# Own rows of the two large groups copied on GpSimd's queue, those of the third made by two products, first one-hots two units later

## Chip, cores and metric

The kernel runs on one NeuronCore of a Trainium2 chip. The metric is the time of one execution in device microseconds (us), lower is better; a measured time is the median of several executions. TensorE is called PE, VectorE DVE, ScalarE ACT, GpSimd POOL and SyncE SP. PE is granted one of two clocks, 2.4 or 1.2 GHz, which the profile shows as 1.00 and 0.50.

## What is computed

Two transformer-like blocks over 256 tokens of width 1024, in float32, each a mixer of attention and recurrence followed by a PEER layer. The change lies in the PEER layer, which both blocks have. For each token it makes queries for 8 heads, scores them against two sets of 128 sub-keys, takes the best 16 of each, then the best 16 of their sums, and so picks 16 of 16384 experts per head. Each expert is one row of `u` and one row of `v`:

```python
q = (xb @ w_q).reshape(B, T, PEER_HEADS, 2, PEER_DKEY // 2)
s1 = jnp.einsum('bthd,nd->bthn', q[..., 0, :], k1); s2 = jnp.einsum('bthd,nd->bthn', q[..., 1, :], k2)
v1, i1 = lax.top_k(s1, PEER_TOPK); v2, i2 = lax.top_k(s2, PEER_TOPK)
...
top_s, pos = lax.top_k(cand_s, PEER_TOPK)
idx = jnp.take_along_axis(cand_i, pos, axis=-1)
g = jax.nn.softmax(top_s, axis=-1)
h = jnp.einsum('bthkd,btd->bthk', jnp.take(u_tab, idx, axis=0), xb)
a = gelu(h) * g
return jnp.einsum('bthk,bthkd->btd', a, jnp.take(v_tab, idx, axis=0))
```

## The kernel before

The function `peer` computes the layer in two ways at once. The first 104 tokens are served by gathered rows. They lie in three groups, `GROUPS = ((2, 0), (4, 64), (16, 96))`: tokens 0 to 63 with each token on 2 partitions, 64 to 95 on 4, and 96 to 103 on 16. POOL fetches the chosen `u` rows and later the `v` rows by indirect DMA, 104 fetches of 128 rows each (512 KB), and DVE multiplies a fetched `u` row with the token's own normed row, which stands in `xg[:, g, :]` on every partition that serves that token (line 1103). The other 152 tokens are served densely: PE multiplies them with all of `u` and all of `v`, and the choice of experts comes in as a gate matrix, made from one-hot rows of the two indices (`one_hots`, `one_hots_by_gate`, `gate_product`, `gate_apply`), in 38 blocks of 4 tokens.

The layer has three stages on PE. In the query stage, 32 units of `w_q` are used: the loop runs `t` over two halves of the tokens and `hc` over 16 halves of heads; each turn multiplies one unit (512 KB of weights, `query`), ACT copies the product into `qts` (line 1332), PE scores the turn before last (`score`, line 1302), and after every second score ACT copies the scores to `s_all` (line 1305). In the `u` stage the dense tokens meet 128 units of `u` (line 1427), with the gate products between them; in the `v` stage they meet 128 units of `v` (line 1484). SP loads all the units in order into seven buffers, as they come free.

The routing (best 16, sums, decoding) is a Python generator that issues DVE work a piece at a time beside the units: `beside` gives it a budget per unit, and a `yield None` ends its turn for that unit. After heads 0 and 1 of the first half it calls `spread`, a few small PE products (line 1147) that bring the expert numbers `eif` (line 1265) onto the partitions of the groups; ACT copies them to `ei`, and POOL may then fetch rows. Three more spreads follow, after each two heads. When the routing has ended (`if not side`), the first block of one-hots is issued at the unit that is then reached; the remaining blocks are spaced evenly up to five units before the end of the stage. Before that a unit may use 0.5 gathered rows, after it 0.98 (`beside(2.45 if at else 2.07, 0.98 if at else 0.5)`). Rows that are not used by then are used in the `v` stage.

Own rows are made in the turns `t == 0`, `hc` 4 to 6: `gain` holds the first half's normed rows (line 1336), and `own_rows` issues 22 DMAs from ACT's queue inside SBUF, 2 of 256 KB, 4 of 128 KB and 16 of 32 KB. ACT issues them in its program's order, between its copies of `q` and of the scores.

Of the kernel before, what the change touches and what calls it, by code (L numbers as in the profile page):

```python
# [12 lines left out]
AF = mybir.ActivationFunctionType  # L13
# [38 lines left out]
def two_blocks_kernel(ctx: ExitStack, tc: tile.TileContext, a: dict, out: bass.AP, dbg=None, stop=None):  # L52
    nc = tc.nc
# [118 lines left out]
    def load_const(pool, name, shape, dt=F32):  # L172
        t = pool.tile(shape, dt, name="c_" + name)
        nc.gpsimd.dma_start(out=t, in_=a[name])
        return t
# [33 lines left out]
    def bank_b(name):  # L209
        return pp_b.tile([P, 512], F32, tag="b", name=name)  # L210
# [788 lines left out]
    def peer(which, norm, names, shared, gelu, after):  # L999
        keys_name, gain_name, u_rows, v_rows = names  # L1000
        with ExitStack() as es:
# [7 lines left out]
            xg = hp.tile([P, len(GROUPS), D], F32, name="xg")  # L1009
# [25 lines left out]
            gain = gp.tile([P, D], F32, tag="rows", name="gain")  # L1035
# [6 lines left out]
            ng = len(GROUPS)  # L1042
            sel = load_const(hp, "sel", [P, ng + sum(c for c in PARTS if c > 1), P])
# [119 lines left out]
            def scales_done(t):  # L1163
                nc.vector.reciprocal(rs[:, t:t + 1], rs[:, t:t + 1])

            def own_rows(g, qs):

                r, t0 = GROUPS[g]
                n = P // r
                for q in qs:  # L1170
                    nc.scalar.dma_start(out=xg[q * n:(q + 1) * n, g, :], in_=gain[t0:t0 + n, :])  # L1171

            def scales_by_column():

# [23 lines left out]
            def route_head(t, h):  # L1198

                for c in range(2):  # L1200
                    yield from best16(v_t[:, c, :], i_t[:, h, t, c, :], s_all[:, h, t, c, :], tmp, 320)
                v1, v2 = v_t[:, 0, :], v_t[:, 1, :]
                for o, a0, na, nb in ((0, 0, 1, 16), (16, 1, 3, 8), (40, 4, 4, 4), (56, 8, 8, 1)):
                    sh = [P, na, nb]
                    nc.vector.tensor_tensor(
                        cand[:, o:o + na * nb].rearrange("p (a b) -> p a b", a=na),
                        bc(v1[:, a0:a0 + na, None], sh), bc(v2[:, None, 0:nb], sh), op=ALU.add)
                yield 660
                yield from best16(top[:, t, h, :], pos[:, t, h, :], cand, tmp[:, 0:64], 270)
# [37 lines left out]
            def exps(t):  # L1247
                nc.vector.tensor_tensor(gt[:, t], top[:, t], bc(top[:, t, :, 0:1], m3), op=ALU.subtract)
                nc.scalar.activation(gt[:, t], gt[:, t], AF.Exp)

            def softmax(t):
                nc.vector.tensor_reduce(zs[:, t], gt[:, t], axis=AX.X, op=ALU.add)
                nc.vector.reciprocal(zs[:, t], zs[:, t])
                nc.vector.tensor_tensor(gt[:, t], gt[:, t], bc(zs[:, t, :, None], m3), op=ALU.mult)

            def routing():

                for h in range(8):
                    while not heads[0]:
                        yield None  # L1260
                    yield from route_head(0, heads[0].pop(0))
                    if h % 2:
                        yield from decode(0, h - 1, 2)
                        hs = slice(h - 1, h + 1)
                        nc.vector.scalar_tensor_tensor(
                            eif, fid[:, 0, 0, hs, :].rearrange("p h k -> p (h k)"), 128.0,
                            fid[:, 1, 0, hs, :].rearrange("p h k -> p (h k)"), op0=ALU.mult, op1=ALU.add)
                        w = G // 4
                        spread(eif, 2, ei[:, (h // 2) * w:(h // 2 + 1) * w])
                        fetch["known"] = h + 1  # L1270
                        fetch_rows()
                exps(0)
                for h in range(8):
                    while not heads[1]:
                        yield None
                    yield from route_head(1, heads[1].pop(0))
                    if h == 0:
                        softmax(0)
                        spread(gt[:, 0].rearrange("p h k -> p (h k)"), 8, gg)
                    if h == 3:  # L1280
                        yield from decode(1, 0, 4)
                exps(1)
                yield from decode(1, 4, 4)
                softmax(1)
                pts = [tpp.tile([P, 512], F32, tag="tp", name="pt") for c in range(2)] + [bank_b("pt")]
                for c, pt in enumerate(pts):
                    for t in range(2):
                        v = gt[:, t] if c == 2 else fid[:, c, t]
                        nc.tensor.transpose(pt[:, t * P:(t + 1) * P], v.rearrange("p h k -> p (h k)"), ident)
                yield None  # L1290
                for c, pt in enumerate(pts):
                    nc.scalar.activation(idx[:, c, :], pt[:, G:T], AF.Copy)

            sps = {}
            heads = [[], []]
# [30 lines left out]
            for t in range(2):  # L1326
                for hc in range(16):
                    q = query(t, hc)
                    if t == 0 and hc == 0:
                        square_sums(x_ss, 0, (1,))  # L1330
                        scales(0)
                    nc.scalar.activation(qts[hc % 4], q, AF.Copy)
                    if t == 0 and hc == 1:
                        scales_done(0)
                        to_plain(1, range(4, 8), norm)
                        nc.vector.scalar_tensor_tensor(gain, x_sb[:, 0, :], rs[:, 0:1], gain, op0=ALU.mult, op1=ALU.mult)
                        side.append(routing())
                    if hc > 1:
                        score(t, hc - 2)
                    elif t == 1:  # L1340
                        score(0, hc + 14)
                    if t == 0 and hc == 2:
                        square_sums(x_ss, 1, (1,))
                        scales(1)
                    if t == 0 and hc == 3:
                        scales_done(1)
                    if t == 0 and hc == 4:
                        own_rows(0, range(2))
                        own_rows(1, range(4))
                    if t == 0 and hc in (5, 6):  # L1350
                        own_rows(2, range(8 * hc - 40, 8 * hc - 32))
                    if t == 1 and hc == 8:
                        by_column = scales_by_column()
                    if t == 1 and 9 <= hc < 13:
                        scaled(by_column, 2 * (hc - 9))
                    beside(2.05, 0.3 * t)
# [74 lines left out]
            for n in range(NE):  # L1431
# [11 lines left out]
                if not side:  # L1443
                    start = at[0] if at else n
# [30 lines left out]
            for n in range(NE):  # L1475
# [7 lines left out]
                for d in range(KT):  # L1483
                    nc.tensor.matmul(  # L1484
                        block(d), lhsT=w[:, d * P:(d + 1) * P], rhs=XA[:, n, :], start=(n == 0 and d % nb == 0),
                        stop=(n == NE - 1), skip_group_check=True)
# [236 lines left out]
```

## Time and profile before

| what | value |
|---|---|
| median of 3 runs | 1810.66 us (1810.16 to 1813.28) |
| the profiled execution | 1809.62 us, of which the span from first to last instruction is 1807.5 us |
| mean granted PE clock | 0.987 |
| busy share of PE, DVE, ACT, POOL | 96%, 63%, 33%, 28% |
| first block: query, `u`, `v` stage on PE | 257.3 to 349.9, 349.9 to 652.3, 652.3 to 936.5 us |
| second block: the same | 1103.7 to 1203.0, 1203.0 to 1505.4, 1505.4 to 1795 us |

Busy shares are means over stages with different limits; the stage in which a thing lies decides what it is worth.

### The profile page before, as it was taken

The numbers are of one execution on the slowest core, as the hardware profiler recorded it, in microseconds if no ns is written. First come the engines' busy times: TensorE is split into PE (matmuls) and PEld (weight loads), VectorE is DVE, ScalarE is ACT, GpSimd is POOL, SyncE is SP. The second block draws the span as 40 slices with busy tenths as digits, with TensorE's granted clock in tenths as the row PEclk, the third lists the DMA queues.
The fourth block names the chain that finished last, engine by engine and source line by source line (L and its number), as shares of the span: only waits on it lengthen the run. The fifth ranks groups of instructions, "written<-read, shape, count | busy, mean of one in ns | idle before, by whom it ended". The sixth has DMA issues, their size and how long they took to land.

```text
span 1807.5 us, 32650 instructions
## 1 busy us (share of the span) xinstructions
PE 1736.6 (96%) x12460; PEld 1625.6 (90%) x12460; DVE 1135.1 (63%) x2698; ACT 594.5 (33%) x1643; POOL 500.1 (28%) x444
## 2 busy tenths in 40 slices
PE   8999996999999999999999998799999999999997
PEld 6778886999999999989988777799999999999997
DVE  5556657798677864445455543879777886444444
ACT  6665541322665520000017563132266651000001
POOL 0000001122344344444410000212244345444441
PEclk9999998999999999999999999799999999999999
DMA  7434568899999999999985227789999999999995
GB/s 267 140 118 139 179 215 275 297 358 396 385 411 418 405 411 419 419 418 419 419 311 186 94 84 251 263 288 367 387 395 412 418 402 419 419 419 419 418 419 219
DMA packets 162732, 591.74 MB, mean 327 GB/s; under 512 B 18528, under 2 KB 18688, under 8 KB 162320
## 3 DMA queue, kind: packets, MB, share of 16 engines
q1 hardware_dynamic: 99648, 362.07, 52.6%
q0 software_dynamic: 61424, 224.12, 31.2%
q10 hardware_dynamic: 1504, 3.48, 0.8%
q8 instruction: 98, 1.61, 0.3%
q14 instruction: 58, 0.48, 0.1%
HBM read 585.40 MB, written 1.05 MB: 324 GB/s over the span
## 4 chain that ended last, share of the span: by engine, by line
PE 75%; DMA 19%; DVE 2%; ACT 1%; issue 1%; ACTq 1%; SPq 0%; DVEq 0%
PE h L1427 29%; DMA raw<-in_v_dram 17%; PE y L1484 14%; PE q L1313 5%; PE pj L296 5%; PE pj L298 5%; PE pj L297 4%; PE g L1387 4%; DMA raw<-in_w_q_dram 2%; PE spread L1147 1%; ACTq L1171 1%; PE sps L1302 1%; PE sc L476 1%; PE hs L797 1%; PE fold L1124 0%
## 5 line engine op out<-in xcount | busy, mean ns | idle before, releaser
L1484 PE MATMUL y<-XA,raw 128*128 128x152 f32 x4096 | 556.6, 295 | 14.4 <-DMA raw<-in_v_dram 10.0
L1484 PEld LDWEIGHTS y<-XA,raw 128*128 128x128 f32 x4096 | 534.2, 190 | 39.3 <-DMA raw<-in_v_dram 34.0
L1427 PE MATMUL h<-un,raw 128*128 128x152 f32 x4096 | 544.0, 293 | 0.0
L1427 PEld LDWEIGHTS h<-un,raw 128*128 128x128 f32 x4096 | 533.0, 190 | 0.0
L1089 POOL DMA_INDIRECT rows<-in_u_rows_dram,ei x208 | 217.7, 1046 | 528.8 <-DVE hg L1103 296.4
L1089 POOL DMA_INDIRECT rows<-in_v_rows_dram,ei x208 | 267.3, 1285 | 316.4 <-DVE acc L1112 251.3
L1112 DVE SCALAR_TENSOR_TENSOR acc<-rows,ag,acc 128x1024 f32<-128x1024 f32 x202 | 259.4, 1284 | 3.1 <-DVE XA L1495 0.3
L1103 DVE CUSTOM_DVE_ANT_0 rows<-rows,xg 128x1024 f32<-128x1024 f32 x208 | 252.7, 1216 | 0.0
L116 ACT ACTIVATE hi<-raw 128x1024 fp32r<-128x1024 f32 (+1 forms) x109 | 114.3, 1052 | 338.7 <-PE y L1484 284.9
L1495 DVE MEMSET XA<- 128x1 f32 x128 | 7.6, 59 | 284.2 <-PE y L1484 258.0
L117 DVE TENSOR_TENSOR lo<-raw,hi 128x1024 fp32r<-128x1024 f32 (+1 forms) x109 | 131.5, 1212 | 84.6 <-ACT hi L116 83.9
L1313 PE MATMUL q<-act,raw 128*128 128x128 f32 x1024 | 138.8, 293 | 5.8 <-issue 5.0
L1313 PEld LDWEIGHTS q<-act,raw 128*128 128x128 f32 x1024 | 132.4, 208 | 6.8 <-issue 5.7
L296 PE MATMUL pj<-hi,act 128*128 128x512 f32 x320 | 131.7, 411 | 2.3 <-ACT hi L116 1.4
L298 PE MATMUL pj<-hi,act_l 128*128 128x512 f32 x320 | 125.8, 393 | 0.1
L297 PE MATMUL pj<-lo,act 128*128 128x512 f32 x320 | 125.7, 393 | 0.0
L1415 ACT ACTIVATE XA<-h 128x152 f32<-128x152 f32 (+37 forms) x252 | 65.4, 260 | 151.5 <-PE h L1427 147.8
L1036 POOL DMA_DIRECT2D gain<-in_gain_dram x2 | 1.1, 534 | 396.5 <-PE out L298 252.6
L1513 ACT ACTIVATE XA<-y 128x384 f32<-128x384 f32 (+1 forms) x6 | 2.5, 456 | 290.3 <-DVE XA L1512 290.3
L1392 DVE TENSOR_TENSOR XA<-g,XA 128x208 f32<-128x208 f32 (+18 forms) x76 | 40.2, 528 | 81.7 <-ACT b L1377 30.2
L1412 ACT ACTIVATE hb<-h 128x8 f32<-128x8 f32 (+37 forms) x152 | 38.2, 251 | 129.6 <-PE h L1427 119.5
L1387 PE MATMUL g<-b,b 128*128 128x128 f32 x608 | 80.1, 275 | 0.0
(367 smaller groups left out, 1814.6 us busy)
## 6 DMA issues: line engine op xcount, KB each, us to landing
raw<-in_u_dram SPq DMA_DIRECT2D x256, 512.0 KB
raw<-in_v_dram SPq DMA_DIRECT2D x256, 512.0 KB
raw<-in_w_in_dram SPq DMA_DIRECT2D x79, 512.0 KB
raw<-in_w_q_dram SPq DMA_DIRECT2D x64, 512.0 KB
raw<-in_w_out_dram SPq DMA_DIRECT2D x16, 512.0 KB
raw<-in_w_mix_dram SPq DMA_DIRECT2D x12, 512.0 KB
rows<-in_u_rows_dram,ei POOLq DMA_INDIRECT x208
rows<-in_v_rows_dram,ei POOLq DMA_INDIRECT x208
```

The source lines that it names most:

```text
L116: nc.scalar.activation(hi[:, c], src[:, c], AF.Copy)
L117: nc.vector.tensor_tensor(lo[:, c], src[:, c], hi[:, c].bitcast(F32), op=ALU.subtract)
L296: nc.tensor.matmul(ps[t], lhsT=ah, rhs=wh[:, j, :], start=(k == 0), stop=False)
L297: nc.tensor.matmul(ps[t], lhsT=ah, rhs=wl[:, j, :], start=False, stop=False)
L298: nc.tensor.matmul(ps[t], lhsT=al, rhs=wh[:, j, :], start=False, stop=(k == last))
L1089: nc.gpsimd.indirect_dma_start(out=t, out_offset=None, in_=tables[c], in_offset=bass.IndirectOffsetOnAxis(ap=ei[:, col[key]:col[key] + 1], ...
L1103: nc.vector.tensor_tensor_reduce(t, t, xg[:, g, :], 1.0, 0.0, ALU.mult, ALU.add, hg[:, k:k + 1])
L1112: nc.vector.scalar_tensor_tensor(acc[g], t, ag[:, k:k + 1], acc[g], op0=ALU.mult, op1=ALU.add)
L1313: nc.tensor.matmul(q, lhsT=w[:, k * P:(k + 1) * P], rhs=acts["x"][:, k, t * P:(t + 1) * P], start=(k == 0), stop=(k == KT - 1))
L1387: nc.tensor.matmul(gs[k][:, j, :], lhsT=b2[:, j, :], rhs=b1[:, j, :], start=True, stop=True)
L1427: nc.tensor.matmul(hs[n], lhsT=w[:, k * P:(k + 1) * P], rhs=un[:, k, :], start=(k == 0), stop=(k == KT - 1))
L1484: nc.tensor.matmul(block(d), lhsT=w[:, d * P:(d + 1) * P], rhs=XA[:, n, :], start=(n == 0 and d % nb == 0), stop=(n == NE - 1), skip_group ...
```

## The change

Six of the 22 copies (groups 0 and 1) are issued from POOL's queue and all at `hc == 4`. The 16 copies of group 2 go: two float32 products with the selection matrix `sel[:, 2, :]` (loaded for the spreads) put the rows into two PSUM banks, and ACT copies each bank (128 x 512) to `xg`. The routing yields twice more at its end, so that the first one-hots come two units later.

```diff
-            def own_rows(g, qs):
+            def own_rows(g):
 
                 r, t0 = GROUPS[g]
                 n = P // r
-                for q in qs:
-                    nc.scalar.dma_start(out=xg[q * n:(q + 1) * n, g, :], in_=gain[t0:t0 + n, :])
+                if r <= 4:
+                    for q in range(r):
+                        nc.gpsimd.dma_start(out=xg[q * n:(q + 1) * n, g, :], in_=gain[t0:t0 + n, :])
+                    return
+                for c in range(2):
+                    cs = slice(c * 512, (c + 1) * 512)
+                    ps = bank_b("xg")
+                    nc.tensor.matmul(ps, lhsT=sel[:, g, :], rhs=gain[:, cs], start=True, stop=True)
+                    nc.scalar.activation(xg[:, g, cs], ps, AF.Copy)
...
                 for c, pt in enumerate(pts):
                     nc.scalar.activation(idx[:, c, :], pt[:, G:T], AF.Copy)
+                yield None
+                yield None
...
                     if t == 0 and hc == 4:
-                        own_rows(0, range(2))
-                        own_rows(1, range(4))
-                    if t == 0 and hc in (5, 6):
-                        own_rows(2, range(8 * hc - 40, 8 * hc - 32))
+                        for g in range(ng):
+                            own_rows(g)
```

The first place is the query stage of the first block, turns `hc` 4 to 7, on ACT (the scratch tiles `qts` and `s_all` lie in `XA`). Before:

```order
L1332 ACTIVATE XA<-q 128x128
L1171 DMA xg<-gain 64x1024 x2
L1171 DMA xg<-gain 32x1024 x4
L1332 ACTIVATE XA<-q 128x128
L1305 ACTIVATE XA<-sps,rs 128x256
L1171 DMA xg<-gain 8x1024 x8
L1332 ACTIVATE XA<-q 128x128
L1171 DMA xg<-gain 8x1024 x8
L1332 ACTIVATE XA<-q 128x128
```

The same place on ACT now (lines are those of the changed file, 9 further on from `query` down):

```order
L1341 ACTIVATE XA<-q 128x128
L1178 ACTIVATE xg<-xg 128x512 x2
L1341 ACTIVATE XA<-q 128x128
L1314 ACTIVATE XA<-sps,rs 128x256
L1341 ACTIVATE XA<-q 128x128 x2
L1314 ACTIVATE XA<-sps,rs 128x256
```

The 22 DMA issues are gone from ACT's order, and two copies from PSUM stand at their first place. On PE, at turns 4 to 6, two products come in between the score of turn 4 and the query of turn 5:

```order
L1322 MATMUL q<-act,raw 128x128 x8
L1311 MATMUL sps<-XA 128x128
L1177 MATMUL xg<-gain,c_sel 128x512 x2
L1322 MATMUL q<-act,raw 128x128 x8
L1311 MATMUL sps<-XA 128x128
```

Everything else of PE's query stage, the spreads too, stands in the same order as before.

The second place is POOL's queue in the first block, from the loads at its start to the end of the row fetches. Before:

```order
L1036 DMA gain<-in_gain_dram 128x1024
L1038 DMA XA<-in_keys_dram 128x256
L174 DMA c_sel<-in_sel_dram 128x896
L174 DMA c_sel_back<-in_sel_back_dram 128x384
L1089 DMA rows<-in_u_rows_dram,ei 128x1024 x104
L1089 DMA rows<-in_v_rows_dram,ei 128x1024 x42
L1477 MEMSET XA 128x1024
L1089 DMA rows<-in_v_rows_dram,ei 128x1024 x62
```

The same stretch of POOL's queue now:

```order
L1036 DMA gain<-in_gain_dram 128x1024
L1038 DMA XA<-in_keys_dram 128x256
L174 DMA c_sel<-in_sel_dram 128x896
L174 DMA c_sel_back<-in_sel_back_dram 128x384
L1172 DMA xg<-gain 64x1024 x2
L1172 DMA xg<-gain 32x1024 x4
L1089 DMA rows<-in_u_rows_dram,ei 128x1024 x104
L1089 DMA rows<-in_v_rows_dram,ei 128x1024 x41
L1484 MEMSET XA 128x1024
L1089 DMA rows<-in_v_rows_dram,ei 128x1024 x63
```

The six copies stand ahead of every row fetch, and one fetch of a `v` row has moved behind the memset that lies in the `v` stage.

The third place is DVE in the `u` stage of the first block, where the routing ends (`rows,hg` is the product of a gathered row, `b` a tile of one-hots, the number behind it only its name). Before:

```order
L1254 TENSOR_TENSOR gt<-gt,XA 128x128
L1103 ISA rows,hg<-rows,xg 128x1024
L1103 ISA hg 128x1
L1366 TENSOR_TENSOR b_3891<-iota,idx 128x512
L1103 ISA rows,hg<-rows,xg 128x1024
```

The same place on DVE now:

```order
L1261 TENSOR_TENSOR gt<-gt,XA 128x128
L1103 ISA rows,hg<-rows,xg 128x1024
L1103 ISA hg 128x1
L1103 ISA rows,hg<-rows,xg 128x1024
L1103 ISA hg 128x1
L1373 TENSOR_TENSOR b_3908<-iota,idx 128x512
```

One row more is used ahead of the first one-hots, which stand two units later; over the two units and the rest of the stage one row fewer is used before the `v` stage begins.

## Rows read from the trace of the kernel before

**Rows 1.** The page: its shares of the chain by line, and the costliest group.

```profile
PE h L1427 29%; DMA raw<-in_v_dram 17%; PE y L1484 14%; PE q L1313 5%; PE pj L296 5%; PE pj L298 5%; PE pj L297 4%; PE g L1387 4%; DMA raw<-in_w_q_dram 2%; PE spread L1147 1%; ACTq L1171 1%; PE sps L1302 1%; PE sc L476 1%; PE hs L797 1%; PE fold L1124 0%
...
L1427 PE MATMUL h<-un,raw 128*128 128x152 f32 x4096 | 544.0, 293 | 0.0
```

**Rows 2.** Timeline, ACT and its queue, first query stage: start, duration, instruction, idle before.

```profile
268.43 10.31 ACTq L1171 DMA_DIRECT2D xg<-gain  x6
278.84 0.28 ACT L1332 ACTIVATE XA<-q 128x128 f32<-128x128 f32 x1 [10.16 <-DMA xg<-gain]
...
280.12 7.04 ACTq L1171 DMA_DIRECT2D xg<-gain  x8
...
287.30 5.33 ACTq L1171 DMA_DIRECT2D xg<-gain  x8
```

**Rows 3.** Timeline of PE, first query stage (x16 is one unit, in two passes).

```profile
266.26 2.05 PE L1313 MATMUL q<-act,raw 128*128 128x128 f32 x16 [0.73 <-DMA raw<-in_w_q_dram]
...
272.39 1.95 PE L1313 MATMUL q<-act,raw 128*128 128x128 f32 x16
279.17 0.80 PE L1302 MATMUL sps<-XA 128*128 128x128 f32 x2 [4.83 <-ACT XA L1332]
...
293.39 1.95 PE L1313 MATMUL q<-act,raw 128*128 128x128 f32 x16
...
295.40 1.40 PE L1147 MATMUL spread<-eif,c_sel 128*128 128x32 f32 x12
...
304.60 0.40 PE L1313 MATMUL q<-act,raw 128*128 128x128 f32 x2 [0.44 <-issue]
...
308.99 3.52 PE L1313 MATMUL q<-act,raw 128*128 128x128 f32 x16
```

**Rows 4.** Timeline of DVE, first block, from the query stage into the u stage.

```profile
261.82 1.28 DVE L1336 SCALAR_TENSOR_TENSOR gain<-x_sb,rs,gain 128x1024 f32<-128x1024 f32 x1 [2.96 <-DMA gain<-in_gain_dram]
...
279.51 0.29 DVE L1187 MAX8 XA<-XA 128x8 f32<-128x128 f32 x1 [8.51 <-ACT XA L1305]
...
291.01 0.19 DVE L1265 SCALAR_TENSOR_TENSOR eif<-XA 128x32 f32<-128x32 f32 x1
...
311.01 1.21 DVE L1103 CUSTOM_DVE_ANT_0 rows<-rows,xg 128x1024 f32<-128x1024 f32 x1
...
332.71 0.47 DVE L1183 TENSOR_TENSOR un<-act,rows 128x304 f32<-128x304 f32 x1 [9.52 <-PE rows L1177]
...
455.87 0.69 DVE L1366 TENSOR_TENSOR b<-iota,idx 128x512 f32<-128x512 f32 x1 [10.25 <-ACT idx L1292]
```

**Rows 5.** Timeline of PE, second query stage.

```profile
1119.42 1.95 PE L1313 MATMUL q<-act,raw 128*128 128x128 f32 x16
...
1147.99 1.78 PE L1147 MATMUL spread<-eif,c_sel 128*128 128x32 f32 x12
```

**Rows 6.** Timeline of PE, first v stage: two float32 products of 128x512, and what follows.

```profile
829.98 1.88 PE L1124 MATMUL fold<-acc,c_sel_back 128*128 128x512 f32 x4
831.70 4.55 PE L1484 MATMUL y<-XA,raw 128*128 128x152 f32 x34
```

**Rows 7.** Groups by line and shape, ACT: a copy of 128x512 from PSUM.

```profile
L718 ACT ACTIVATE kkT<-pt 128x512 f32<-128x512 f32 x2 | 1.2, 594 | 1.5 <-PE pt L717 1.5
```

**Rows 8.** Timeline of POOL, first block: the first row fetch.

```profile
297.48 0.99 POOL L1089 DMA_INDIRECT rows<-in_u_rows_dram,ei  x1 [37.57 <-ACT ei L1156]
```

**Rows 9.** Busy time of PE, PEld, DVE, ACT, POOL by stretch; clock, DMA share, GB/s.

```profile
268.00:284.00 16.00, 10.55 (x75) 10.06 (x74) 6.97 (x45) 0.92 (x3) 0.00 (x0) 0.82 0.99 304
285.00:290.00 5.00, 2.40 (x11) 2.40 (x12) 4.62 (x14) 0.28 (x1) 0.00 (x0) 0.50 0.47 136
...
330.00:350.00 20.00, 18.28 (x163) 18.09 (x163) 16.60 (x64) 5.41 (x23) 2.10 (x3) 1.00 0.78 257
...
680.00:900.00 220.00, 213.48 (x1545) 201.68 (x1545) 103.80 (x129) 0.00 (x0) 101.75 (x79) 1.00 1.03 419
1540.00:1740.00 200.00, 193.29 (x1404) 183.09 (x1403) 94.67 (x118) 0.00 (x0) 91.96 (x72) 1.00 1.03 419
```

## The prediction

> **What bounds it now.** I read the chain that ended last first, then the timelines of PE, ACT, DVE and POOL in the query stage, then the same in the second block, then busy time by stretch. The chain is PE for most of the span and the loads of `v` for 17% [rows 1]; ACT's queue, line 1171, is on it with 1% only. That share misleads. It counts the last link, and the stage where line 1171 stands loses more. ACT spends 10.31, 7.04 and 5.33 us on 6, 8 and 8 copies of own rows [rows 2], and in that time issues no copy of `q`. PE, which scores `q` two turns later, stands idle before the scores, 4.83 us before the first [rows 3]. A turn of the query stage takes 2.01 us with its score (293.39 to 295.40), so the three turns `hc` 7, 8 and 9 should take 6.0 us; they take 21.0 us, from 272.39 to 293.39 [rows 3]. A part of that is the clock, which falls to 0.50 after the idle time [rows 9]. The same stands in the second block.
>
> Two things end the gain at a floor. The first is DVE, which makes the routing of heads 0 and 1 before the first `spread`. It waited 8.51 us for the scores of head 1, began at 279.51 and had `eif` 11.69 us later, at 291.01 + 0.19 [rows 4]. The second is the DMA queues: in the `v` stages of both blocks they run at share 1.03 and 419 GB/s [rows 9], and PE waits for `v`. Every byte that moves into a `v` stage costs time there. In the `u` stage it is PE: line 1427 has no idle time before it in either block [rows 1].
>
> **The copies, first block.** What goes from ACT is 22 issues, 22.7 us of its queue [rows 2]. What comes to PE's path is two float32 products of 128 x 512. The fold makes the same two: from 829.98 the next work begins at 831.70, so 1.72 us [rows 6]. ACT's two copies from PSUM take 0.59 us each [rows 7] and lie beside PE's next unit, since `q` of that turn is needed two turns later; without that cover they would cost 1.2 us.
>
> The new order then runs as follows. Turn 4 starts at 266.26 as now, and its query with score lasts to 268.4 [rows 3]. The two products take PE to 270.1. Turn 5 with the score that completes head 1 ends at 272.1. ACT copies the scores to `s_all`, and DVE begins; now it begins 0.67 us after ACT comes free (278.84 to 279.51) [rows 2, 4], so I take 0.6 us: 272.7. With 11.7 us of work [rows 4], `eif` is there at 284.4. PE itself would reach the spread after turn 10, which is 270.1 plus six turns of 2.01, at 282.2; it waits 2.2 us for DVE. The spread starts at 284.5 instead of 295.40 [rows 3]: 10.9 us earlier.
>
> Behind the spread the order is the old one, and I let all of it move up by 10.9 us. DVE stands closer to PE there: its next head now begins when ACT comes free at 292.6 [rows 2], ahead of the spread, and would begin just at it. That is covered. DVE is ahead enough to wait 9.52 us for PE in this stage [rows 4], and it would cost PE only if more than that were lost. The slow stretch behind the first spread stays in the sum: the unit at 308.99 should have come at 304.8, PE is held for no reason that the profile shows [rows 3], while eight row fetches fill the queues; then it runs one unit in 3.52 instead of 1.95 us. Together 5.8 us in each block. The burst comes just as close to the spread as before.
>
> **The copies, second block.** Turn 5 began at 1119.42 [rows 5]. With the products 1121.1, with its score 1123.1, DVE from 1123.7, `eif` at 1135.4, spread at 1135.5 instead of 1147.99 [rows 5]: 12.5 us. DVE's work per pair of heads is taken from the first block.
>
> **POOL's queue.** The six copies wait for `gain`, ready at 261.82 + 1.28 = 263.1 [rows 4]; behind them wait only the row fetches, of which the first now starts at 297.48 [rows 8] and would start near 286.6. No row shows a copy inside SBUF issued by POOL. Its nearest row, an indirect fetch, takes 0.99 us [rows 8]: six take 6 us and end at 269. From 263.1 to the spread 21 us are free, so three times that price would still be hidden; the bounds are 0 and 0 up to there, and the fourth rival has the case beyond. I take no cost.
>
> **The transfers.** Group 2 loses its 16 small DMAs; 1 MB of copies stays and now starts near 264 instead of 269, where PE had just waited 0.73 us for a weight unit [rows 3]. The weights come in beside them: from 268 to 284 the queues moved 304 GB/s in all [rows 9], so if half goes to weights, a unit of 0.524 MB takes 3.45 us while the copies last, 1.05 MB / 152 GB/s = 6.9 us. In that time two units land and PE could use 3.4. At worst PE is 1.4 turns, 2.9 us, late; 2.2 us of that would fall into the wait for `eif`, unless turn 5 itself is late and shifts DVE. Bounds: 0 and 3 us per block. I take 0, because the units for turns 4 and 5 were asked for before the copies. The Trainium skill, page "DMA: Bandwidth & Descriptors", section "Issuing engines are not separate DMA queues", says that DMAs started by any engine share the same 16 engines and that another issuer saves only issue time, which it calls usually small. The trace agrees on the sharing (304 GB/s with the copies, 419 without) and not on the size, with 22.7 us of issue on ACT. By the rule the copies would be worth about nothing, which is the second rival below.
>
> **The one-hots.** PE's products in the `u` stage are the same in number, each block three units behind its one-hots as before. They begin two units later and stand on neighbouring units at two places per block; PE has no idle time there [rows 1], and the 10.25 us for which DVE waits for `idx` [rows 4] hide behind it. So nothing is won on PE. But for two units 0.5 instead of 0.98 rows are used, and one row fetch per block moves into the `v` stage, as the order shows. There 0.524 MB at 419 GB/s [rows 9] cost 1.25 us, 2.5 us for both blocks. The bounds are 0, if the queues have room before that stage, and 2.5 us per block for two rows; I take one row.
>
> **The sum.** 10.9 + 12.5 - 2.5 = 20.9 us off the profiled execution's 1809.6, that is 1788.7 us; the median of the runs is 1.0 us above it, so I say 1789.8 us, 1.15% less.
>
> **Rivals.** *Weights are late after all.* The copies take the queues when PE has no unit in hand, and the burst of eight row fetches comes with fewer units loaded than now, when PE's stall lets all seven buffers fill (share 0.47 in the stall) [rows 9]. Costs of 3 us for the copies and 2 to 3 us in the burst per block leave 9 to 11 us: about 1800 us. For it speaks the wait of 0.73 us; against it that a turn takes 2.01 us and a unit alone 1.25 us. Chance 0.12.
>
> *The queues take it all back.* The `v` stage is bound by bytes; if they are never idle before it, PE's earlier arrival only turns into longer waits for `v`, and the moved row comes on top: 1810.7 + 2.5 = 1813 us. Against it: from 330 to 350 the share is 0.78 [rows 9], so what was missed can be caught up before the `u` stage. Chance 0.06.
>
> *The slow stretch behind the spread goes.* If PE's unexplained stops came from buffers that were full when the burst began, they may vanish: up to 5.8 us more per block, 1778 us. Nothing shows their cause. Chance 0.07.
>
> *The other side: POOL is slow with these copies.* If the six copies land late, the row product on DVE, at 311.01 now [rows 4] and near 300 then, waits for `xg`, and behind it on DVE the routing of the next heads, on which the next spreads wait. DVE has some 6 us to spare there, so it decides against the change from the point where `xg` lands 6 + 11 us after 300, at 317, which is 54 us after the issue; 65 us would give about 1830 us. Against it: ACT's queue spent 24 us from the first of 22 copies to the end of the last issue, 268.43 to 292.63 [rows 2], other work between them. A rule speaks for this rival: the Trainium skill, page "SBUF — State Buffer", section "Summary: rules for kernel authors", advises to issue from ACT or SP beside DVE work, because GpSimd cannot write its descriptors while DVE, in its faster modes, holds the port that the two share. No run here shows it for such copies. Chance 0.03.
>
> **The numbers.** My forecast has 0.72, with 1783 to 1796 as its own range (3 us per block either way for the transfers and the start of DVE). Faster by over 0.2% holds it, the late weights and the vanished slow stretch: 0.91. Same 0.06, slower 0.03; 0.2%, or 3.6 us, is about what a measurement of this kernel can tell from no change. The range of 1781 to 1800 leaves out most of the vanished stretch, half of the late weights, and the two last cases.
>
> **What would show it.** Right: no line of `xg` on ACT's queue; turns 6 to 9 in steps of 2.0 us at clock 1.00; a wait of about 2 us before the first spread in both blocks, ended by `eif` line 1265; first spread near 284.5, second block's query stage 21 to 23 us earlier, with the first block's `v` stage 1 us longer. Wrong: waits of PE for `raw<-in_w_q_dram` in turns 5 to 14; the `v` stage longer by the same 10 us by which the query stage is shorter; waits of DVE for `xg`; waits of PE between gate products where blocks stand on neighbouring units.

## The result, and the profile after

The changed kernel takes 1790.31 us, the median of 4 runs (1787.17 to 1792.32), beside 1811.97 us for the kernel before (4 runs); the ratio is 0.9876 with a 95% interval of 0.9852 to 0.9900. The forecast was 1789.8 us. The profiled execution took 1787.17 us, its span 1785.1 us.

PE in the first query stage, from the timeline (start, duration, instruction, idle before it and what ended that), answers to [rows 3]; line 1313 of before is line 1322 now:

```profile
265.94 2.05 PE L1322 MATMUL q<-act,raw 128*128 128x128 f32 x16
268.05 1.88 PE L1177 MATMUL xg<-gain,c_sel 128*128 128x512 f32 x4
269.77 1.95 PE L1322 MATMUL q<-act,raw 128*128 128x128 f32 x16
...
274.65 2.05 PE L1322 MATMUL q<-act,raw 128*128 128x128 f32 x16 [0.71 <-DMA raw<-in_w_q_dram]
277.89 2.05 PE L1322 MATMUL q<-act,raw 128*128 128x128 f32 x16 [0.96 <-DMA raw<-in_w_q_dram]
...
284.25 1.51 PE L1147 MATMUL spread<-eif,c_sel 128*128 128x32 f32 x12
...
293.66 0.38 PE L1322 MATMUL q<-act,raw 128*128 128x128 f32 x2 [0.98 <-issue]
295.07 0.40 PE L1322 MATMUL q<-act,raw 128*128 128x128 f32 x2 [1.03 <-issue]
297.20 0.59 PE L1322 MATMUL q<-act,raw 128*128 128x128 f32 x2 [1.72 <-issue]
...
299.58 3.62 PE L1322 MATMUL q<-act,raw 128*128 128x128 f32 x16
```

The three holes in front of the scores are gone. The two products take 1.72 us (268.05 to 269.77), PE waits 0.71 and 0.96 us for weights, and reaches the spread at 284.2; from the last turn's start at 282.01 the stage runs without a gap into it. Behind it stands the slow stretch of before again, PE issuing two products per 1.4 us.

DVE in the same stage answers to [rows 4], POOL to [rows 8]:

```profile
262.24 1.28 DVE L1345 SCALAR_TENSOR_TENSOR gain<-x_sb,rs,gain 128x1024 f32<-128x1024 f32 x1 [3.08 <-DMA gain<-in_gain_dram]
...
272.49 0.29 DVE L1194 MAX8 XA<-XA 128x8 f32<-128x128 f32 x1 [1.17 <-ACT XA L1314]
284.00 0.19 DVE L1272 SCALAR_TENSOR_TENSOR eif<-XA 128x32 f32<-128x32 f32 x1
...
303.88 1.21 DVE L1103 CUSTOM_DVE_ANT_0 rows<-rows,xg 128x1024 f32<-128x1024 f32 x1
```

```profile
263.82 2.98 POOL L1172 DMA_DIRECT2D xg<-gain  x6 [3.61 <-DVE gain L1345]
286.43 1.00 POOL L1089 DMA_INDIRECT rows<-in_u_rows_dram,ei  x1 [19.63 <-ACT ei L1156]
```

DVE now waits 1.17 us for head 1's scores, not 8.51, begins at 272.49 and has `eif` at 284.19. POOL issues the six copies in 2.98 us and then stands idle for 19.63 us. The first row product on DVE, at 303.88, does not wait for `xg`.

PE in the second query stage answers to [rows 5]:

```profile
1109.62 2.05 PE L1322 MATMUL q<-act,raw 128*128 128x128 f32 x16 [0.19 <-DMA raw<-in_w_q_dram]
1112.96 2.05 PE L1322 MATMUL q<-act,raw 128*128 128x128 f32 x16 [1.07 <-DMA raw<-in_w_q_dram]
1115.68 2.05 PE L1322 MATMUL q<-act,raw 128*128 128x128 f32 x16 [0.44 <-DMA raw<-in_w_q_dram]
...
1124.20 1.50 PE L1147 MATMUL spread<-eif,c_sel 128*128 128x32 f32 x12 [0.21 <-DVE eif L1272]
```

Busy time by stretch (PE, PEld, DVE, ACT, POOL, then clock, DMA share, GB/s) answers to [rows 9]; from 268 to 284 PE is busy for 14.34 us, not 10.55, at clock 1.00, not 0.82:

```profile
268.00:284.00 16.00, 14.34 (x114) 12.99 (x113) 13.69 (x66) 3.95 (x11) 0.00 (x0) 1.00 1.02 333
285.00:290.00 5.00, 5.00 (x46) 5.00 (x46) 4.62 (x30) 2.32 (x12) 2.91 (x3) 1.00 0.81 278
...
680.00:900.00 220.00, 213.52 (x1544) 201.53 (x1543) 105.00 (x130) 0.00 (x0) 102.79 (x80) 1.00 1.03 419
```

The table gives the stages of one profiled execution of each kernel, read off the first and last rows of the timelines of PE: the two query stages from the first `q` to the first `h`, in brackets the first spread's start after the stage's start; the two `v` stages from the first `y` to the last. (The first `v` stage of the kernel before ends with its last `y` at 942.3 us; the 936.5 in the table of the kernel before is wrong.) The `u` stage is 302.27 us in every one. The four comparisons did not run on one chip, and the last column is the median of the kernel before in the same comparison, so times are compared as ratios to it.

| kernel | query 1 | query 2 | `v`, both blocks | ratio to before [95%] | before, us |
|---|---|---|---|---|---|
| before | 92.57 (38.06) | 99.28 (44.28) | 579.76 | 1 | 1811.97 |
| changed | 83.08 (26.61) | 85.92 (29.92) | 580.19 | 0.9876 [0.9852, 0.9900] | 1811.97 |
| rows_only | 77.07 (26.67) | 83.23 (31.21) | 577.56 | 0.9844 [0.9823, 0.9865] | 1803.0 |
| onehots_only | 90.98 (40.68) | 96.45 (43.78) | 580.54 | 1.0005 [0.9994, 1.0017] | 1803.0 |
| all_pool | 79.86 (26.44) | 82.19 (30.96) | 580.45 | 0.9901 [0.9880, 0.9922] | 1803.0 |
| six_on_act | 87.65 (34.82) | 90.97 (37.61) | 581.31 | 0.9978 [0.9965, 0.9990] | 1803.0 |
| changed_again | 78.55 (26.53) | 83.46 (31.44) | 581.56 | 0.9873 [0.9858, 0.9888] | 1802.32 |
| onehots_8 | 76.94 (26.54) | 79.04 (30.27) | 588.34 | 0.9912 [0.9896, 0.9928] | 1802.32 |
| no_burst | 76.96 (26.58) | 84.36 (32.34) | 576.88 | 0.9855 [0.9837, 0.9873] | 1802.32 |
| rows_no_burst | 77.18 (26.79) | 83.80 (31.78) | 577.80 | 0.9892 [0.9877, 0.9906] | 1802.32 |
| rows_only_2 | 83.24 (26.37) | 87.87 (31.32) | 579.97 | 0.9851 [0.9829, 0.9874] | 1812.99 |
| rows_spread | 78.98 (26.25) | 84.67 (32.07) | 575.75 | 0.9809 [0.9790, 0.9827] | 1812.99 |
| thin_copies | 82.71 (26.35) | 89.16 (32.77) | 580.71 | 0.9855 [0.9835, 0.9876] | 1812.99 |
| all_products | 84.68 (30.07) | 91.22 (34.83) | 580.91 | 0.9913 [0.9896, 0.9930] | 1812.99 |

### The profile page after: what moved, and what is told of

Read it like the earlier page. It is cut to its first block, busy times and chain, and to the rows that moved or that the text cites. A ratio compares the mean times of both kernels' runs of the same rounds, so it can differ in the third digit from the quotient of the medians.

```text
span 1785.1 us, 32628 instructions
## 1 busy us (share of the span) xinstructions
PE 1730.7 (97%) x12468; PEld 1617.5 (91%) x12468; DVE 1135.8 (64%) x2694; ACT 597.4 (33%) x1643; POOL 509.5 (29%) x456
## 4 chain that ended last, share of the span: by engine, by line
PE 75%; DMA 18%; DVE 3%; issue 2%; ACT 1%; SPq 0%; ACTq 0%; DVEq 0%
PE h L1434 30%; DMA raw<-in_v_dram 16%; PE y L1491 15%; PE pj L296 5%; PE pj L298 5%; PE q L1322 5%; PE pj L297 5%; PE g L1394 4%; DMA raw<-in_w_q_dram 1%; PE spread L1147 1%; PE sc L476 1%; PE hs L797 1%; PE sps L1311 1%; DMA x_sb<-in_x_dram 0%; PE o L296 0%
## 5 line engine op out<-in xcount | busy, mean ns | idle before, releaser
L1089 POOL DMA_INDIRECT rows<-in_u_rows_dram,ei x208 | 223.8, 1076 | 489.1 <-DVE hg L1103 271.5
L1089 POOL DMA_INDIRECT rows<-in_v_rows_dram,ei x208 | 263.6, 1268 | 318.2 <-DVE acc L1112 248.5
L1322 PE MATMUL q<-act,raw 128*128 128x128 f32 x1024 | 132.2, 283 | 11.1 <-issue 7.6
L1322 PEld LDWEIGHTS q<-act,raw 128*128 128x128 f32 x1024 | 125.0, 198 | 14.6 <-issue 9.2
L1422 ACT ACTIVATE XA<-h 128x152 f32<-128x152 f32 (+36 forms) x252 | 65.9, 262 | 159.6 <-PE h L1434 153.0
L1399 DVE TENSOR_TENSOR XA<-g,XA 128x216 f32<-128x216 f32 (+18 forms) x76 | 40.6, 535 | 83.5 <-PE g L1394 33.1
L1419 ACT ACTIVATE hb<-h 128x4 f32<-128x4 f32 (+36 forms) x148 | 36.8, 249 | 121.1 <-PE h L1434 110.9
```

The source lines that it names most:

```text
L1089: nc.gpsimd.indirect_dma_start(out=t, out_offset=None, in_=tables[c], in_offset=bass.IndirectOffsetOnAxis(ap=ei[:, col[key]:col[key] + 1], ...
L1322: nc.tensor.matmul(q, lhsT=w[:, k * P:(k + 1) * P], rhs=acts["x"][:, k, t * P:(t + 1) * P], start=(k == 0), stop=(k == KT - 1))
```

## The experiments

### The change in its two halves

**rows_only** is the changed kernel without the two units ahead of the one-hots, **onehots_only** the kernel before with nothing but these:

```diff
                 for c, pt in enumerate(pts):
                     nc.scalar.activation(idx[:, c, :], pt[:, G:T], AF.Copy)
-                yield None
-                yield None
```

> The changed kernel without the two later units (own rows as changed, one-hots as before). If the copies carry the gain, both query stages are as short as in the changed kernel (83.1 and 85.9 us against 92.6 and 99.3). If a row that moves into the v stage costs its bytes there, as the forecast had it, each v stage is 1.25 us shorter than in the changed kernel and the time is 2.5 us below it, about 1787.5 us on a median; if the row costs nothing the time is that of the changed kernel, 1790 us. Rival: the later one-hots carry part of the gain; then this kernel is slower than the changed one by more than 2 us, and a stage says where.

> The kernel before with the two later units alone. Forecast: query and u stages as before (92.6, 302.3 and 99.3, 302.3 us), each v stage 1.25 us longer, 1813 to 1814.5 us. If the row costs nothing: 1811 to 1812 us, each v stage within 0.6 us of before. Rival (the later one-hots take a wait of DVE away that counts): faster than before by 2 us or more.

The rows carry the whole gain: 0.9844 alone, while the two units alone come to 1.0005. The first spread stands 26.67 us after the stage's start in rows_only, as in the changed kernel.

**rows_only_2** is the same kernel again on another chip.

> The changed kernel without the two units ahead of the one-hots, a second time, beside the other three on one chip. Row-byte theory: 0.9845 to 0.986 of the kernel before, 2 to 4 us below the changed kernel's 0.9873, the difference in the v stages. Rival (the first comparison was one of chips): 0.987 to 0.988.

It came to 0.9851, as the row-byte theory had it. The changed kernel's two ratios are 0.9876 and 0.9873, so the two units cost 2 to 3 thousandths by the ratios, 4 to 6 us, and 0.9 us (-1.1 to +3.1) by onehots_only. The intervals overlap, and a cost near the forecast's 2.5 us fits both.

### Which engine issues, and how many copies

**six_on_act** leaves group 2 to the products and puts the other six copies back on ACT's queue:

```diff
-                        nc.gpsimd.dma_start(out=xg[q * n:(q + 1) * n, g, :], in_=gain[t0:t0 + n, :])
+                        nc.scalar.dma_start(out=xg[q * n:(q + 1) * n, g, :], in_=gain[t0:t0 + n, :])
```

> The changed kernel with the six large copies issued from ACT again, the third group by products as in the change. If issue time on ACT is the cost, ACT is held for some 10 us from 268 on (the six took 10.3 and 8.6 us before), head 1's scores reach DVE near 278.5 instead of 272.4, eif comes near 290, and the first spread lies about 6 us later than in the changed kernel in each block: about 1800 to 1803 us. If the 16 small copies were the whole cost, or the bytes and not the issuer, the time is that of the changed kernel, 1790 us.

ACT, its queue and DVE in its first query stage:

```profile
269.39 10.97 ACTq L1172 DMA_DIRECT2D xg<-gain  x6
280.41 1.08 ACT L1178 ACTIVATE xg<-xg 128x512 f32<-128x512 f32 x2 [10.77 <-DMA xg<-gain]
```

```profile
282.06 0.30 DVE L1194 MAX8 XA<-XA 128x8 f32<-128x128 f32 x1 [9.40 <-ACT XA L1314]
```

The same six DMAs hold ACT's queue for 10.97 us and POOL's for 2.98 us, and DVE then waits 9.40 us for scores that ACT can't copy. The ratio falls back to 0.9978. So of the changed kernel's gain the issuer of the six copies makes 0.0105 (0.9978 - 0.9873, ratios from two chips), 19 us; the expectation, 10 to 13 us, was too low. For the sixteen small copies onehots_only is the kernel to compare with, as it ran on the same chip and has the same two units: six_on_act is 5.4 us faster (1798.47 to 1803.82), which is what the small copies cost while the six stand on ACT too. The Trainium skill, page "DMA: Bandwidth & Descriptors", section "Issuing engines are not separate DMA queues", has it that another issuer saves only issue time and that this is usually small relative to the DMA itself; here it is worth 19 us, as the engine that issued was one for whose copies two others waited.

**all_pool** makes no products and issues all 22 copies from POOL:

```diff
-                if r <= 4:
+                if r <= 16:
```

> The changed kernel with the 16 small copies of the third group on GpSimd's queue too, and no products for own rows. If issue time on ACT was the cost, and GpSimd issues one copy in 0.5 us (six took 2.98 us), 22 issues take 11 us there and hide; DVE's eif comes up to 1.7 us earlier, but 0.5 MB more of copies beside the weights hold PE longer, so each query stage is within 2 us of the changed kernel's: 1788 to 1794 us. If GpSimd is slow with such copies (the forecast's rival), its first row fetch starts later than 286.4 us and DVE waits for xg: above 1795 us.

POOL, then PE, in its first query stage:

```profile
266.07 4.01 POOL L1172 DMA_DIRECT2D xg<-gain  x8 [3.63 <-DVE gain L1345]
274.88 0.50 POOL L1172 DMA_DIRECT2D xg<-gain  x1 [4.80 <-DMA xg<-gain]
```

```profile
273.22 2.05 PE L1322 MATMUL q<-act,raw 128*128 128x128 f32 x16 [0.80 <-DMA raw<-in_w_q_dram]
276.79 2.05 PE L1322 MATMUL q<-act,raw 128*128 128x128 f32 x16 [1.29 <-DMA raw<-in_w_q_dram]
280.18 2.05 PE L1322 MATMUL q<-act,raw 128*128 128x128 f32 x16 [1.11 <-DMA raw<-in_w_q_dram]
```

0.9901. After eight issues at 0.50 us POOL waits 4.80 us for the first copies to land, and goes on one at a time. PE waits 3.2 us for weights and meets the spread 26.44 us after the stage's start, where the changed kernel is too. The products and the sixteen small copies cost about the same up to there. Behind the spread PE goes on waiting for weights:

```profile
293.03 2.05 PE L1322 MATMUL q<-act,raw 128*128 128x128 f32 x16 [1.19 <-DMA raw<-in_w_q_dram]
```

There it waits 2.6 us in the first block and 1.0 in the second, which changed_again below does not. The whole is 5 us above the changed kernel by the ratios (0.9901 and 0.9873), with intervals that just overlap.

**all_products** goes the other way: all three groups by products, no copy inside SBUF, by taking out the branch for `r <= 4`.

> The changed kernel with all three groups' rows made by products: no copies inside SBUF at all, four more products of 128x512 and four more copies out of PSUM per block. By the rows: 4 x 0.86 us, 3.4 us more on TensorE in front of the first spread, and 4 x 0.59 us on ScalarE. Theory (a 2.2 us slack at the spread, of which the weights took 1.7): without the copies the weights' 1.7 us is gone, so the products have 2.2 us to hide in and 1 to 2 us per block are left, +2 to +4 us in all against the changed kernel. Rival (the copies' transfers cost more than shows): equal or up to 3 us faster than the changed kernel, with more of the v and query stages undisturbed.

0.9913, 7 us above the changed kernel's 0.9873, and both expectations were wrong. DVE shows why:

```profile
275.17 0.29 DVE L1190 MAX8 XA<-XA 128x8 f32<-128x128 f32 x1 [4.63 <-ACT XA L1310]
```

PE's product of turn 5 and head 1's second score stand behind the products, and DVE, the floor, begins 4.63 instead of 1.17 us late. So four products more shift `eif` by their full 3.5 us (4.63 - 1.17); PE then waits 2.26 us at the spread, and nothing hides in that wait. It also tells that the changed kernel's own products are not all free: DVE's 1.17 us there is theirs (all_pool, without products, has no such wait, and `eif` 25.25 us after the stage's start against 26.55).

### The weights

**thin_copies** issues the same six copies with 64 of the 1024 columns, and fills the rest with ones:

```diff
-                        nc.gpsimd.dma_start(out=xg[q * n:(q + 1) * n, g, :], in_=gain[t0:t0 + n, :])
+                        nc.gpsimd.dma_start(out=xg[q * n:(q + 1) * n, g, :64], in_=gain[t0:t0 + n, :64])
+                    if g == 1:
+                        nc.gpsimd.memset(xg[:, 0:2, 64:], 1.0)
```

> The changed kernel with the six copies on GpSimd's queue cut to 64 of the 1024 columns (the other columns of xg's first two groups are set to one, so xg is not the reference's): the same issues, a sixteenth of the bytes. Theory (the copies' transfers hold up the weights in front of the first spread by some 1.7 us, and the wait for eif hides it): the waits for raw in the first query turns fall from 1.7 us to under 0.5, TensorE's wait for eif at the spread rises to about 2, the first spread stays within 0.4 us of the changed kernel's 26.5 us after the query's start, and the kernel's time is equal within 0.1% or 1 to 2 us shorter by what the weights gain later. Rival (the weights set the spread): the spread comes 1.5 us earlier per block, 3 us in all.

PE at its first spread:

```profile
281.57 1.95 PE L1324 MATMUL q<-act,raw 128*128 128x128 f32 x16
283.36 0.39 PE L1313 MATMUL sps<-XA 128*128 128x128 f32 x2
286.00 2.73 PE L1147 MATMUL spread<-eif,c_sel 128*128 128x32 f32 x12 [2.26 <-DVE eif L1274]
```

As the first theory said: in the first block no wait for weights is left before the spread, the wait for `eif` is 2.26 us, and the spread stands 26.35 us after the stage's start, not 26.5. With 15/16 of the copies' bytes gone the first spread gains nothing. (In the second block it stands at 32.77, behind a third and a fourth turn that ran slowly, in 3.62 and 2.77 us, so that block can't be compared.) The ratio, 0.9855, can't be told from the changed kernel's. One thing it did lose: after the 2.26 us of idle time the spread runs in 2.73 instead of 1.51 us, and the clock from 285 to 290 us is 0.59.

### The row fetches behind the one-hots

**onehots_8** has eight units instead of two:

```diff
-                yield None
-                yield None
+                for _ in range(8):
+                    yield None
```

> The changed kernel with eight units instead of two ahead of the one-hots. Row-byte theory (each 2 MB row fetch that is moved out of the query products into the v stage costs its 1.25 us of the DMA there): the first spread comes about three heads later, some two or three row fetches per block move, so +5 to +8 us against the changed kernel, all of it in the v stages. Rival (the v stage does not notice): 0, or a gain from fewer transfers beside the weights of the query. Third possibility: the spread becomes later than the fold needs and the DVE waits, then the query stage, not v, is longer by more than 1 us per block.

The spread stays where it was (26.54 us; that part of the expectation was wrong). Three more row fetches per block stand in the `v` stage (99, not 96, counted in POOL's timeline), and it is 6.8 us longer in both blocks together, 1.13 us for a fetch of 0.524 MB (not 2 MB, as the expectation says), where 419 GB/s make 1.25. The whole is 5.6 us slower (1785.91 to 1780.36), within the 5 to 8 us expected. The bytes do cost their time there.

### The slow stretch

**changed_again** is the changed kernel itself, on a chip where the kernel before takes 1802.32 us.

> The changed kernel itself, so that the three beside it are compared with it on one chip. By the result so far: 0.988 of the kernel before. rows_only, the same without the two units for the one-hots, came to 0.9844 in another comparison: if the one-hots' two units cost what the forecast said (one row fetch per block in the v stage, +2.5 us), this kernel lies 2 to 3 us above that, near 0.986; if they cost what the onehots_only run showed (nothing), the two are equal within 0.2%, and the difference between 0.988 and 0.9844 is one of chips.

Its ratio is 0.9873, and its PE has no slow stretch. From the spread on:

```profile
285.31 1.50 PE L1147 MATMUL spread<-eif,c_sel 128*128 128x32 f32 x12 [0.39 <-DVE eif L1272]
...
296.80 1.95 PE L1322 MATMUL q<-act,raw 128*128 128x128 f32 x16
298.59 0.39 PE L1311 MATMUL sps<-XA 128*128 128x128 f32 x2
298.81 1.95 PE L1322 MATMUL q<-act,raw 128*128 128x128 f32 x16
```

The same program, the same eight row fetches, and every turn takes 2.01 us; the query stage is 78.55 instead of 83.08 us. In the two comparisons in which the kernel before takes 1802 to 1803 us none of the eight kernels profiled shows waits for issue there; in the two in which it takes 1812 to 1813 us all six do, before and after too. So the stretch goes with the chip, or with what the chip was doing, and not with the kernel, as far as one profile of each can tell. The DMA queues differ with it. Packets, MB and share by queue from 285 to 300 us, in the changed kernel's first profile and then in changed_again (q0 is the row fetches', q1 the weights'):

```profile
q0 software_dynamic: 1088, 4.00, 70.3%
q1 hardware_dynamic: 411, 1.47, 24.3%
```

```profile
q1 hardware_dynamic: 846, 3.07, 50.3%
q0 software_dynamic: 649, 2.40, 43.1%
```

Which is cause and which effect these rows don't tell: a PE that stops frees no weight buffer, and in that window SP issued 4 units in the first and 7 in the second.

**no_burst** holds the row fetches back after the first spread:

```diff
-            fetch = {"known": 0, "issue": 0, "use": 0, "goal": 0.0}
+            fetch = {"known": 0, "issue": 0, "use": 0, "goal": 0.0, "cap": 1}
...
-                    if key[1] >= fetch["known"]:
+                    if key[1] >= fetch["known"] or n >= fetch["cap"]:
...
+                if fetch["known"] and fetch["issue"] < 2 * G:
+                    fetch["cap"] += 0.5
+                    fetch_rows()
...
                     if t == 1 and hc == 8:
+                        fetch["cap"] = 2 * G
```

> The changed kernel with the row fetches behind the first spread held to one per two units of the query, instead of eight in 10 us; the same rows in the end, none left out. Theory A: the slow stretch behind the first spread (TensorE issuing two products per 1.4 us, named issue, 291.7 to 299.6 us in block 1) is the burst of row fetches holding up the fetch of TensorE's own instructions; spread out, the stretch goes, and the query is 5 to 8 us shorter per block, 10 to 15 in all. Rival B: the stretch has another cause (it is absent in rows_only, which has the same burst); then nothing is gained, and if row fetches are moved into v the kernel is slower by up to 1.25 us for each.

> The rows of xg as changed, the one-hots as before, and the row fetches spread out as in no_burst. By theory A (the burst causes the slow stretch): equal to no_burst or 2 to 3 us faster. By rival B: at most the time of rows_only (0.984 of the kernel before), which shows no such stretch in its first block.

no_burst came to 0.9855, 4.1 us below changed_again, but the intervals overlap, and on this chip there was no stretch to remove: theory A was not tested. rows_no_burst is not the kernel that its expectation describes. Its edit took two other `yield None` out, in the mixer, and left the one-hots' two in; it is no_burst with 7.0 us more between the two blocks' layers (160.54 to 167.55 us), a median 6.4 us higher (1782.70 to 1776.28), and says nothing of the one-hots.

**rows_spread** is the kernel that rows_no_burst's expectation describes: the rows as changed, no extra units, the fetches held back as in no_burst. It ran beside rows_only_2 on a chip with the stretch.

> What rows_no_burst was meant to be: the rows of xg as changed, no extra units ahead of the one-hots, row fetches held to one per two units of the query. In rows_no_burst the two units were taken from another place, the mixer between the blocks, whose gates then started sooner and whose trace is 6.7 us longer there; it kept the one-hots' two units. If spreading the fetches is a gain of its own (no_burst against the changed kernel: 4 us), this one is 2 to 4 us below rows_only_2; if what no_burst gained is only what rows_only gains too (a v stage of 288.5 instead of 290.5 us), the two are equal.

It is the fastest of all, 0.9809, 8.1 us below rows_only_2 (1778.54 to 1786.64), where 2 to 4 us were expected. The waits of PE over the whole span, rows_only_2 first (total, times, longest):

```profile
PE y L1489 <- DMA raw<-in_v_dram: 11.0, 33, 1.7
PE q L1320 <- issue: 6.1, 7, 1.7
```

```profile
PE y L1493 <- DMA raw<-in_v_dram: 7.9, 29, 1.1
...
PE q L1320 <- issue: 2.1, 4, 1.0
```

The waits for issue fall from 6.1 to 2.1 us and the two query stages by 7.5 us; the `v` stages are 4.2 us shorter, as in no_burst (4.7 us). The first fetches still come close together, six from 287.47 to 293.77 us instead of eight, so this was a smaller cut of the burst than its expectation says. It supports the first half of theory A for the chips that have the stretch: fewer row fetches in a row, shorter stops. How much shorter is rough: thin_copies and all_products, on the same chip with all eight fetches, have PE waits for issue of 4.3 and 5.5 us behind the first spreads. What stops PE is not shown. The other half names the loading of PE's instructions; the two queues that the profile calls instruction (q8, q14) have no packet from 288 to 306 us in the changed kernel's first profile, in which PE stops from 292.7 to 298, so a late load is not seen there.

## Why the prediction was right

**The first spread.** Forecast 284.5 with `eif` at 284.4; measured 284.25 and 284.19, in a stage that began 0.31 us later. The 0.6 us by which it is better come ahead of the products: turn 4 did not wait again the 0.73 us for weights that the forecast had kept [rows 3], and the change has no part in that. In every kernel that issues none of these copies from ACT and makes two products or none, the spread stands 26.25 to 26.79 us after the stage's start. DVE is not the floor in all of them: PE, late by its weights, comes out at nearly the same time, and in all_pool, where `eif` is there at 25.25, PE alone sets the spread.

**The two products.** 1.72 us forecast and measured, ACT's copies 0.60 us each. That they lie on DVE's path and not only on PE's was in the working (turn 5 after 270.1); all_products shows it at three times the size.

**The weights.** Taken as 0, with bounds of 0 and 3 us. The units were late, by 0.71 and 0.96 us in the first block and 0.19, 1.07 and 0.44 in the second, so the rival had a true mechanism; but PE's forecast wait of 2.2 us for `eif` covered it, as the working said it would, and little of that wait is left (0.21 us in the second block). thin_copies takes the bytes away and finds the 2.26 us again. The rival's gain of only 9 to 11 us is refuted. Two of the signs named beforehand misled: waits for weights in turns 7 and 8, a sign of being wrong, did come, and the wait of 2 us before the spread, a sign of being right, did not, because the late weights filled it.

**The second block.** 12.5 us forecast; from 44.28 to 29.92 us after the stage's start it is 14.4. The first score and turns 3 and 4 of that stage, from PE's timeline, first of the kernel before and then of the changed one:

```profile
1113.48 0.46 PE L1302 MATMUL sps<-XA 128*128 128x128 f32 x2 [3.81 <-issue]
1113.78 2.83 PE L1313 MATMUL q<-act,raw 128*128 128x128 f32 x16
1116.82 2.54 PE L1313 MATMUL q<-act,raw 128*128 128x128 f32 x16
```

```profile
1103.23 0.46 PE L1311 MATMUL sps<-XA 128*128 128x128 f32 x2 [3.00 <-DMA XA<-in_keys_dram]
1103.52 1.95 PE L1322 MATMUL q<-act,raw 128*128 128x128 f32 x16
1105.53 1.95 PE L1322 MATMUL q<-act,raw 128*128 128x128 f32 x16
```

The forecast took turn 5's place as it was, behind a wait of 3.81 us and these slow rows (1.5 us for the two). In the changed kernel's profile the wait, named there as one for the sub-keys, is 0.8 us shorter and the rows are not slow. Neither comes with the change each time: in changed_again, the same program, the wait is 3.35 us and turn 3 is slow again:

```profile
1100.38 3.51 PE L1322 MATMUL q<-act,raw 128*128 128x128 f32 x16
```

There the spread stands 31.44 us after the stage's start, 12.8 us less than in the kernel before. So the forecast of this block was about right, and most of the 1.9 us on top in the profiled execution are luck.

**The slow stretch.** Kept in the sum at its size, it became 1.95 and 1.0 us longer (first spread to first `h`: 54.51 to 56.46, 55.00 to 55.99). The rival in which it goes was wrong for this change; it goes on another chip.

**The one-hots.** One fetch per block moved as forecast (96, not 95, in the `v` stage). The term of 2.5 us is the one that was off in the profiled pair: the `v` stages grew by 0.43 us. Over all kernels, the seven with the two units and no cap on fetches have `v` stages of 580.2 to 581.6 us, the three without 577.6 to 580.0; that is about 1.7 us between the means, a rough size, as the three lie 2.4 us apart. onehots_8 confirms the price per byte. The term has the right mechanism and about two thirds of its size.

**POOL and the queues that take it back.** POOL needed 2.98 us for the six issues, and nothing waited for `xg`. The rule of the Trainium skill that stood for that rival (page "SBUF — State Buffer", section "Summary: rules for kernel authors") holds for DVE in its faster modes. Such a cost does not show here: all_pool's issue at 274.88, in the middle of DVE's work, takes the 0.50 us that each of the first eight takes; no run shows in which mode DVE was. The `v` stages did not grow by what the query stages lost, so the queues did not take it back.

The parts from the profile: -11.45 and -14.36 us up to the spreads, +1.95 and +1.0 behind them, +0.43 in `v`, together -22.4, the difference of the spans (1807.5 to 1785.1). The forecast's -20.9 came from -23.4 and +2.5. The spreads came 2.4 us earlier than forecast, the slow stretch, kept as it was, got 2.95 us longer, and the `v` stages grew by 2.1 us less. That these misses leave only 1.5 us is in part luck; the mechanism, ACT's queue freed and DVE as the next limit, is the one forecast.

## What to carry to other kernels

A queue's share of the critical chain (1% for line 1171) says little of what its issuer's delay is worth: look at what the engine doesn't do while it issues, and who waits for that. Before pricing new work on an engine, find the slack at the place where the next engine takes over; work ahead of the slower engine's input (the products ahead of DVE's scores) doesn't get that slack, work beside it (late weights) does. Compare kernels on one chip: here the chips differ by 10 us, half of what the change is worth.

## What was not expected

The slow stretch of 5 us per block is a matter of the chip or its state: with one program the row fetches' queue took 70% of the 16 DMA engines' time in one run and 43% in another, from 285 to 300 us, and only in the first did PE stop. DVE stops in the same microseconds, between instructions of its own, and ACT copies the `q` of the turn that PE ended at 291.5 only at 298.00, as these rows of the changed kernel show:

```profile
295.08 0.18 DVE L1226 TENSOR_SCALAR XA<-XA 128x32 uint32<-128x32 uint32 x1 [0.84 <-DVE XA L1202]
298.00 0.51 ACT L1341 ACTIVATE XA<-q 128x128 f32<-128x128 f32 x2 [9.62 <-remote]
```

And spreading out a few row fetches in the query stage made the `v` stages, 300 us later, 4 us shorter on two chips, although the same number of fetches (96 in no_burst as in changed_again) stands there. Why, stays open.
